# Query and key weights of the second attention in chunks for four heads, with the norm's weights applied while they are split

## The chip, the core and the metric

The kernel runs on one core of one Trainium2 chip. A core has a matrix engine (TensorE, "PE" in the profile, with its weight loads "PEld"), a vector engine (VectorE, "DVE"), a scalar engine (ScalarE, "ACT"), GpSimd ("POOL") and SyncE ("SP"), which here issues nearly all DMAs. Each engine works through its own instructions in order and waits on semaphores where it needs another's result. SBUF is the working memory of 128 partitions, and matmul results land in eight PSUM banks. The metric is the device time of one execution in microseconds.

## The reference

A trunk of two layers on 512 tokens of 1024 features: latent attention and a SwiGLU feed-forward, then chunked attention and a second feed-forward. The change touches the second attention alone. It has 16 heads of 64 features; its keys and values come from the same residual stream as its queries, under a norm with other weights:

```python
def shared_kv(x, g_src, w_kv):
    kv = (rms_norm(x, g_src) @ w_kv).reshape(B, S, 2, B_HEADS, B_HEAD_DIM)
    return gather_band(kv[:, :, 0]), gather_band(kv[:, :, 1])

def chunked_mixer(h, k_band, v_band, w_q, rel_table, w_o):   # h = rms_norm(x, attn_pre_g[1])
    q = (h @ w_q).reshape(B, n_c, CHUNK, B_HEADS, B_HEAD_DIM)
    ...
    s = jnp.einsum('bnqhd,bnkhd->bnhqk', q, k_band, preferred_element_type=jnp.float32)
    s = s * (B_HEAD_DIM ** -0.5) + bias[None, None]
    s = jnp.where(valid[None, :, None, None, :], s, -jnp.inf)
    p = jax.nn.softmax(s, axis=-1).astype(v_band.dtype)
    o = jnp.einsum('bnhqk,bnkhd->bnqhd', p, v_band).reshape(B, S, B_HEADS * B_HEAD_DIM)
    return o @ w_o
```

The norm is `x * rsqrt(mean(x^2)) * g`. The kernel multiplies the weight matrix's rows by `g` and the projection's result by the reciprocal root, so that the projections can run on `x` itself.

## The kernel before, in words

**Precision.** Every product of two float32 matrices is made of three matmuls on parts: a number is split into a high part (a cast, line 144, ScalarE) and the rest (a subtraction, line 145, VectorE), and `mm3` (lines 361 to 363) adds high x high, low x high and high x low. Where a gain goes in with the split, `split_scaled` does the same with a scaled copy and a scalar-tensor-tensor operation (lines 148 and 149).

**Weights.** `Feed` holds one list of all weight chunks of the program, up to 128 x 1024 each. A chunk is loaded by SP into one of five `raw` tiles (line 287), split into `whi` and `wlo` (three of each), and used by TensorE. `feed.next` takes the next chunk, and `feed.ahead` starts the split of the one after it. For query and key weights a chunk is one 128-feature tile of outputs over all eight input tiles of 128, so each of its eight column blocks has its own gain; line 309 multiplies the whole raw tile in place on VectorE before the split.

**The second attention.** Heads go in pairs; a pair is 128 features. `fill_b` is a generator of filler: each step, called a unit here, is one `mm3` of 512 columns for a query or key projection, or later for the output projection. A pair takes eight units for its queries and eight for its keys, then yields its number, a mark that counts as a step too. Behind the eighth unit the result is scaled by the reciprocal root (line 1582), split, and written by 4 or 8 DMAs of SP (line 1588) into the tiles `q1`, `k1` and `k2` of the pair, which lie in a ring of six.

`attention` runs 16 heads x 4 query tiles = 64 slots. Slot `i` of a head with query tile `qt` takes 128 x (`qt` + 1) keys: two score matmuls (lines 1634 and 1635, tile `sc`), one VectorE step that adds the bias and finds the minimum (line 509), and one exponential on ScalarE (line 511). Two slots later TensorE transposes the result (line 523, tile `pt`), and ScalarE and VectorE split it into `pth` and `ptl`. When a head's four tiles are there, its value product follows (lines 1642 and 1643), then `ot` and `of` (lines 1648 and 1649); after the second head of a pair the sums are turned into reciprocals, spread over a tile (`rw`, line 1654), transposed (line 1663), multiplied in and split into `oh` and `ol`. Between these steps `weave` lets the filler run up to a count: the first 12 units at slot 0, then evenly so that `units` are used up in slot 64. The filler's last part, the output projection of the attention (`out_first_b`), needs the finished pair `k` before its step `k`: three units for each of the first seven pairs inside the slots, and seven more units that are kept for behind the last scores.

The first pair's projections run ahead of the attention, between the two halves of the value projection (`plan_v`). The bias of a head is a 256 KB load on SP (line 1565) into a ring of three, begun when the head before starts, and a small memset on GpSimd.

A scheduler puts instructions of all engines in order when the program is built, so a DMA or a split can stand ahead of work written before it.

Of the kernel before, what the change touches and what calls it, by code (L numbers as in the profile page):

```python
# [18 lines left out]
D, S, P = 1024, 512, 128  # L19
# [49 lines left out]
def trunk(ctx: ExitStack, tc: tile.TileContext, a, out):  # L69
# [16 lines left out]
    def U(dt=F32, name="u"):  # L86
        return up.tile([P, S], dt, tag="u", name=name_(name), bufs=NU)
# [4 lines left out]
    def bank(tag="mm", name="b"):  # L92
        return ps.tile([P, S], F32, tag=tag, name=name_(name), bufs={"mm": 4, "s": 2, "t": 2}[tag])
# [41 lines left out]
    @contextmanager  # L135
    def first(n):

        tc.cur_priority -= n
        yield
        tc.cur_priority += n  # L140


    def split(dst_hi, dst_lo, src):
        return (nc.scalar.copy(dst_hi, src),  # L144
                V.tensor_tensor(dst_lo, src, dst_hi.bitcast(F32), op=OP.subtract))  # L145

    def split_scaled(dst_hi, dst_lo, src, col):
        return (nc.scalar.activation(dst_hi, src, AF.Copy, scale=col),
                V.scalar_tensor_tensor(dst_lo, src, col, dst_hi.bitcast(F32), op0=OP.mult, op1=OP.subtract))
# [102 lines left out]
    class Feed:  # L252
# [37 lines left out]
        def split(self, i):  # L290
            while len(self.ready) <= min(i, len(self.plan) - 1):
                j = len(self.ready)
                self.load(j + 2)
                raw, (src, n, gain, room) = self.raw[j], self.plan[j]
                for f in range(j, min(j + 8, len(self.plan))):
                    if f < j + 5 and isinstance(self.plan[f][0], Pair) or isinstance(self.plan[f][0], Down):
                        self.load(f)
                if isinstance(src, Down):
                    src.sums(*gain)
                    raw = src.at[gain]  # L300
                elif isinstance(src, Pair):
                    src.sums(gain)
                    raw = src.raw[gain]
                elif gain is not None and gain.shape[1] > 2:
                    rv = raw[:, :n].rearrange("p (a b) -> p a b", a=gain.shape[1])
                    with ExitStack() as st:
                        for b in self.behind.get(j, ()):
                            st.enter_context(tc.issue_after(b.ins))
                        V.tensor_tensor(rv, rv, gain, op=OP.mult)
                    gain = None  # L310
                if room is None:
                    at_ = 24 if isinstance(src, Pair) else 0
                    pieces = [tuple(wp.tile([P, 1152], F32R, tag=t, name=name_("w" + t), bufs=3)[:, at_:at_ + 1024]
                                    for t in ("hi", "lo"))]
                else:
                    pieces = self.room[room]()
                w = pieces[0][0].shape[1]
                if isinstance(raw, list):
                    c = 0
                    for t in raw:  # L320
                        c_ = slice(c, c + t.shape[1])
# [38 lines left out]
    def mm3(o, l, r, start, stop):  # L360
        nc.tensor.matmul(o, l[0], r[0], start=start, stop=False)  # L361
        nc.tensor.matmul(o, l[0], r[1], start=False, stop=False)  # L362
        last_mm[0] = nc.tensor.matmul(o, l[1], r[0], start=False, stop=stop)  # L363
        return last_mm[0]
# [163 lines left out]
    def attention(n_heads, start, fill, first, units, after, pace=()):  # L528


        pace = list(pace)
        slots = n_heads * NQT
        heads, done, late = {}, [0], []
        rate = (units - first) / slots

        def weave(upto):
            n = 0
            most = pace.pop(0) if fill.scored and pace else 4
            while (n < most if fill.scored else done[0] < upto) and fill.step():
                done[0] += 1  # L540
                n += 1

        for i in range(slots + 3):
            h, qt = divmod(i, NQT)
            if h < n_heads:
                if qt == 0:
                    heads[h] = start(h)
                    if h == 0:
                        weave(first)
                heads[h].scores(qt)  # L550
                fill.scored = i == slots - 1
# [12 lines left out]
        if late:  # L564
            late.pop()()
# [209 lines left out]
    plan_out(w_o[1], KT, True)  # L775
    plan_ffn(1)

# [783 lines left out]

    def bias(h):

        bt = biases[h] = pool[0].tile([P, S], F32, tag="bias", name=f"bias_{h}", bufs=3)
        nc.sync.dma_start(bt, bass.AP(tensor=rel.tensor, offset=rel.offset + h * L, ap=[[1, P], [1, S]]))
        nc.gpsimd.memset(bt[:64, :64], -BIG)

    def fill_b():
        for pr in range(H_B // 2):
            q1, k1, k2 = (pool[0].tile([P, 2, S], F32R, tag="st", name=f"{n}_{pr}", bufs=6) for n in ("q1", "k1", "k2"))  # L1570
            for t in range(2):
                b = bank()
                w = feed.next(1024, False)
                for k in range(KT):
                    if k == 3:
                        feed.ahead()
                    mm3(b, w(k * P, P), xs[k], k == 0, k == KT - 1)
                    yield True
                l = U(name="f")
                h = U(F32R, "fh")  # L1580
                with first(50):
                    V.tensor_tensor(l, b, rb, op=OP.mult)
                    split(h, l, l)
                h = h.bitcast(F32)
                for e, own in enumerate((LO, HI)):
                    for d, src, rows in (((k1, h, LO), (k1, h, HI), (k2, l, LO), (k2, l, HI)) if t else
                                         ((q1, h, LO), (q1, l, HI))):
                        nc.sync.dma_start(d[rows, e].bitcast(F32), src[own])
            qk_b[pr] = q1, k1, k2
            yield pr  # L1590
        yield from out_first_b()

    def out_first_b():
# [116 lines left out]
def _layout(i):  # L1710
# [20 lines left out]
        for f in range(2)])  # L1731
# [24 lines left out]
    o["w_qkb"] = np.stack([np.stack([_chunks(w, r(j * P, j * P + P), KT)[0] for w in (wq, wkv)])  # L1756
                           for j in range(H_B // 2)])

    w = np.clip(r(S + P - 1) - CHUNK, 0, MAX_REL + CHUNK - 1)
    o["rel"] = c(i["b_rel_table"][0][:, w])  # L1760
# [23 lines left out]
```

## Time and profile before

| | |
|---|---|
| median of three runs | 1115.44 us (1115.43 to 1116.55) |
| profiled execution, first to last instruction (its span) | 1112.9 us |
| mean granted TensorE clock | 0.998 |
| TensorE busy, matmuls | 1100.7 us, 99% |
| VectorE busy | 931.1 us, 84% |
| ScalarE busy | 685.6 us, 62% |
| first scores of the second attention | 588.8 us from the start |
| scores of its last slot | 732.9 us from the start |

The profile gives no time for the profiled execution beyond its span; the runs' times lie about 2.5 us above it. In rows of the trace, a name like `whi<-raw` is the written tile and what it is made from; "idle before" is the time the engine stood still just ahead of the instructions of a group. Matmuls overlap: the time from one start to the next is what TensorE spends on one, and its duration is longer.

### The profile page before, as it was taken

To read this page: it belongs to the slowest core of one execution; us is meant where nothing else is said; L and a number is where in the kernel's file an instruction comes from. 1 tells how busy PE (TensorE), PEld (TensorE's weight loads), DVE (VectorE), ACT (ScalarE), POOL (GpSimd) and SP (SyncE) were. 2 spreads that over 40 slices of the span, in tenths; PEclk is the share of its full clock that TensorE was granted. 3 is DMA by queue.
4 is the path that set the end of the run, shared out by engine and by line. 5 is a ranking of instruction groups with operands and counts; after the bars stand their busy time and mean duration, and the time that the engine had idled before them with its cause. 6 is when DMAs were issued, how large, how long until landed. Compare 5 with 4: busy or idle time off the path is not lost.

```text
span 1112.9 us, 18983 instructions
## 1 busy us (share of the span) xinstructions
PE 1100.7 (99%) x6973; PEld 983.8 (88%) x6973; DVE 931.1 (84%) x1671; ACT 685.6 (62%) x1339; POOL 68.5 (6%) x106
## 2 busy tenths in 40 slices
PE   9999999999999999999999999999999999999997
PEld 6888889999999998888888888889999999998885
DVE  7788737999989889978868878658999899889977
ACT  6576637755555556768636777666755555566675
POOL 1200000000000002400000000000000000002402
PEclk9999999999999999999999999999999999999999
DMA  7433226423332358970556665635422322459923
GB/s 237 117 107 81 72 72 213 133 73 108 95 125 96 126 168 240 148 213 28 186 152 170 156 181 146 152 121 176 141 76 95 133 81 97 137 170 294 172 55 77
DMA packets 62990, 150.85 MB, mean 136 GB/s; under 512 B 8432, under 2 KB 10224, under 8 KB 62896
## 3 DMA queue, kind: packets, MB, share of 16 engines
q1 hardware_dynamic: 55552, 136.61, 39.0%
q0 software_dynamic: 6912, 12.59, 6.9%
q8 instruction: 55, 0.90, 0.3%
q10 hardware_dynamic: 432, 0.44, 0.1%
q14 instruction: 39, 0.32, 0.1%
HBM read 119.52 MB, written 9.63 MB: 116 GB/s over the span
## 4 chain that ended last, share of the span: by engine, by line
PE 91%; DVE 3%; DMA 2%; issue 1%; ACT 1%; POOL 0%; SPq 0%; POOLq 0%; DVEq 0%; ACTq 0%
PE al L1487 17%; PE b L361 11%; PE b L362 11%; PE b L363 11%; PE be L1487 9%; PE al L1237 8%; PE be L1237 5%; PE ga L1487 4%; PE de L1237 3%; PE ga L1237 3%; PE pt L523 2%; DMA x<-in_x 1%; DVE wlo L145 1%; PE b L1643 1%; PE b L1642 1%
## 5 line engine op out<-in xcount | busy, mean ns | idle before, releaser
L144 ACT CAST whi<-raw 128x1024 fp32r<-128x1024 f32 (+3 forms) x224 | 225.2, 1007 | 203.8 <-PE al L1487 72.2
L145 DVE TENSOR_TENSOR wlo<-raw,whi 128x1024 fp32r<-128x1024 f32 (+3 forms) x224 | 260.6, 1165 | 52.2 <-ACT whi L144 51.3
L1487 PE MATMUL al<-th,whi 128*128 128x256 f32 x432 | 122.8, 284 | 0.2 <-DVE ut L1499 0.2
L1487 PE MATMUL al<-tl,whi 128*128 128x256 f32 x432 | 120.8, 280 | 0.0
L1487 PE MATMUL al<-th,wlo 128*128 128x256 f32 x432 | 120.8, 280 | 0.0
L361 PE MATMUL b<-xh,whi 128*128 128x512 f32 (+1 forms) x298 | 114.5, 385 | 0.0
L363 PE MATMUL b<-xh,wlo 128*128 128x512 f32 (+1 forms) x298 | 110.0, 369 | 0.3 <-DVE wlo L145 0.3
L362 PE MATMUL b<-xl,whi 128*128 128x512 f32 (+1 forms) x298 | 109.9, 369 | 0.0
L174 DVE TENSOR_TENSOR raw<-raw,raw 128x1024 f32<-128x1024 f32 x72 | 86.4, 1217 | 0.6 <-DMA raw<-in_w_pair 0.4
L1487 PEld LDWEIGHTS al<-th,whi 128*128 128x128 f32 x432 | 81.2, 188 | 2.5 <-DVE ut L1499 0.5
L1487 PEld LDWEIGHTS al<-tl,whi 128*128 128x128 f32 x432 | 81.3, 188 | 0.0
L1487 PEld LDWEIGHTS al<-th,wlo 128*128 128x128 f32 x432 | 81.2, 188 | 0.1
L511 ACT ACTIVATE p<-p,mn 128x128 f32<-128x128 f32 (+1 forms) x96 | 54.0, 562 | 39.5 <-DVE mn L509 38.6
L145 DVE TENSOR_TENSOR ptl<-pt,pth 128x128 fp32r<-128x128 f32 (+1 forms) x96 | 46.6, 486 | 29.4 <-ACT pth L144 23.6
L145 DVE TENSOR_TENSOR wlo<-wd,whi 128x512 fp32r<-128x512 f32 x86 | 56.4, 684 | 14.4 <-ACT whi L144 14.2
L144 ACT CAST whi<-wd 128x512 fp32r<-128x512 f32 x86 | 50.0, 619 | 25.5 <-PE al L1237 10.6
L363 PEld LDWEIGHTS b<-xh,wlo 128*128 128x128 f32 x298 | 56.2, 189 | 10.0 <-DVE wlo L145 0.7
L361 PEld LDWEIGHTS b<-xh,whi 128*128 128x128 f32 x298 | 56.4, 189 | 6.4 <-ACT whi L144 0.4
L362 PEld LDWEIGHTS b<-xl,whi 128*128 128x128 f32 x298 | 56.5, 189 | 5.6
L144 ACT CAST pth<-pt 128x128 fp32r<-128x128 f32 (+1 forms) x96 | 40.2, 420 | 26.9 <-PE pt L523 26.1
L1237 PE MATMUL al<-whi,ph 128*128 128x512 f32 x132 | 51.7, 392 | 0.0
L1237 PE MATMUL al<-whi,pl 128*128 128x512 f32 x132 | 51.6, 391 | 0.0
(315 smaller groups left out, 3272.0 us busy)
## 6 DMA issues: line engine op xcount, KB each, us to landing
raw<-in_w_pair SPq DMA_DIRECT2D x72, 512.0 KB, 3.7
wd<-in_w_down SPq DMA_DIRECT2D x54, 256.0 KB, 5.9
raw<-in_w_o SPq DMA_DIRECT2D x16, 512.0 KB, 3.5
raw<-in_w_gu SPq DMA_DIRECT2D x16, 512.0 KB, 3.7
raw<-in_w_down SPq DMA_DIRECT2D x16, 512.0 KB, 4.4
raw<-in_w_qkb SPq DMA_DIRECT2D x16, 512.0 KB, 3.7
wd<-in_w_down POOLq DMA_DIRECT2D x22, 256.0 KB, 5.5
wd<-raw POOLq DMA_DIRECT2D x22, 256.0 KB, 4.4
```

The source lines that it names most:

```text
L144: return (nc.scalar.copy(dst_hi, src), V.tensor_tensor(dst_lo, src, dst_hi.bitcast(F32), op=OP.subtract))
L145: V.tensor_tensor(dst_lo, src, dst_hi.bitcast(F32), op=OP.subtract))
L174: V.tensor_tensor(t, x, y, op=OP.add)
L361: nc.tensor.matmul(o, l[0], r[0], start=start, stop=False)
L362: nc.tensor.matmul(o, l[0], r[1], start=False, stop=False)
L363: last_mm[0] = nc.tensor.matmul(o, l[1], r[0], start=False, stop=stop)
L511: nc.scalar.activation(p[:, :n], p[:, :n], AF.Exp, bias=mn[:, :1], scale=-1.0, accum_out=self.sums[:, qt:qt + 1])
L523: nc.tensor.transpose(t[:, kt * P:(kt + 1) * P], p[:, kt * P:(kt + 1) * P], ident)
L1237: nc.tensor.matmul(to[e], l[c], r[d], start=j < 4 and k == 0 and n == 0, stop=k == NF // 2 - 1 and n == 2, skip_group_check=True)
L1487: nc.tensor.matmul(o, l[c], r[d], start=first_ and n == 0, stop=k == K2 - 1 and n == 2, skip_group_check=True)
L1642: nc.tensor.matmul(o[:, q_], vv, pth[:, kt, q_], start=kt == 0, stop=False)
L1643: nc.tensor.matmul(o[:, q_], vv, ptl[:, kt, q_], start=False, stop=kt == NQT - 1)
```

## The change

The query and key weights of four heads (two pairs) are laid out as four chunks: two for the queries, two for the keys, each of four input tiles of 128 by 256 output columns. A column block of 256 then has one gain, and the chunk's four blocks are split with `split_scaled` in place of line 309 and the plain split. `fill_b` makes four heads at a time with two PSUM banks, half of the input tiles per chunk. The filler before the attention is now the four heads' 32 units. The ring of `q1`, `k1`, `k2` grows from six to nine tiles, the bias ring shrinks from three to two, and the number of units given to `attention` is written as `12 + 4 * H_B * 2`, which is 140 like the number before.

```diff
-                elif gain is not None and gain.shape[1] > 2:
-                    rv = raw[:, :n].rearrange("p (a b) -> p a b", a=gain.shape[1])
...
-                        V.tensor_tensor(rv, rv, gain, op=OP.mult)
-                    gain = None
...
-                        for d in range(0, m, S):
-                            split_scaled(pieces[c // w][0][:, d:d + S], pieces[c // w][1][:, d:d + S],
-                                         raw[:, c + d:c + d + S], gain[:, (c + d) // S, 0:1])
+                        step = n // gain.shape[1]
+                        for d in range(0, m, step):
+                            split_scaled(pieces[c // w][0][:, d:d + step], pieces[c // w][1][:, d:d + step],
+                                         raw[:, c + d:c + d + step], gain[:, (c + d) // step, 0:1])
...
-    def plan_pair(pr):
+    def plan_four(n):
+        gv = gqk.rearrange("p (k t) -> p k t", t=2)
         for t in range(2):
-            feed.add(a["w_qkb"][pr, t], 1024, gqk[:, t::2].unsqueeze(2).to_broadcast([P, KT, P]))
+            for kc in range(2):
+                feed.add(a["w_qkb"][n, t, kc], 1024, gv[:, 4 * kc:4 * kc + 4, t:t + 1])
 
     plan_v(0)
-    plan_pair(0)
+    plan_four(0)
     plan_v(1)
-    for pr in range(1, H_B // 2):
-        plan_pair(pr)
+    for n in range(1, H_B // 4):
+        plan_four(n)
...
-        bt = biases[h] = pool[0].tile([P, S], F32, tag="bias", name=f"bias_{h}", bufs=3)
+        bt = biases[h] = pool[0].tile([P, S], F32, tag="bias", name=f"bias_{h}", bufs=2)
...
     def fill_b():
-        for pr in range(H_B // 2):
-            q1, k1, k2 = (pool[0].tile([P, 2, S], F32R, tag="st", name=f"{n}_{pr}", bufs=6) for n in ("q1", "k1", "k2"))
+        for n in range(H_B // 4):
+            st_ = {}
             for t in range(2):
-                b = bank()
-                w = feed.next(1024, False)
-                for k in range(KT):
-                    if k == 3:
-                        feed.ahead()
-                    mm3(b, w(k * P, P), xs[k], k == 0, k == KT - 1)
-                    yield True
...
+                b = [bank() for _ in range(2)]
+                for kc in range(2):
+                    w = feed.next(1024, False)
+                    for j in range(2):
+                        if j:
+                            feed.ahead()
+                        for kk in range(4):
+                            k = 4 * kc + kk
+                            mm3(b[j], w(kk * 256 + j * P, P), xs[k], k == 0, k == KT - 1)
+                            yield True
+                        if not kc:
+                            continue
+                        names = ("k1", "k2") if t else ("q1",)
+                        st_[t, j] = [pool[0].tile([P, 2, S], F32R, tag="st", name=f"{m}_{2 * n + j}", bufs=9)
+                                     for m in names]
...
+            for j in range(2):
+                qk_b[2 * n + j] = st_[0, j][0], *st_[1, j]
+            yield 2 * n
+            yield 2 * n + 1
         yield from out_first_b()
...
-    attention(H_B, start_b, fill, 12, 7 * 17 + 21, True, (0, 1, 1, 1, 1, 2, 4))
+    attention(H_B, start_b, fill, 12, 12 + 4 * H_B * 2, True, (0, 1, 1, 1, 1, 2, 4))
```

Two places of the instructions' order are of use. The first is TensorE late in the attention, before the change, from the scores of slot 56 (`sc_8354`) to those of slot 57; `b_8282` to `b_8284` are the banks of the output projection, that is filler, and `pt` is the transposed tile of slot 54:

```order
L1634 MATMUL sc_8354<-k_7_8038,q_7_8037 128x128
L361 MATMUL b_8284<-oh_7293,whi_8319 128x512
L1635 MATMUL sc_8354<-k_7_8039,q_7_8037 128x128
L362 MATMUL b_8284<-ol_7294,whi_8319 128x512
L363 MATMUL b_8284<-oh_7293,wlo_8320 128x512
L523 MATMUL pt_8364<-ident,p_8291 128x128 x3
L361 MATMUL b_8282<-oh_7519,whi_8198 128x512
L362 MATMUL b_8282<-ol_7520,whi_8198 128x512
L363 MATMUL b_8282<-oh_7519,wlo_8199 128x512
L1634 MATMUL sc_8373<-k_7_8038,q_7_8037 128x256
```

With the change, the same place from the scores of slot 55 (`sc_8469`) to the transposes of slot 55's result (`pt_8505`), behind the scores of slot 58; lines stand six lower:

```order
L1640 MATMUL sc_8469<-k_6_8112,q_6_7868 128x512
L1641 MATMUL sc_8469<-k_6_8113,q_6_7868 128x512
L517 MATMUL pt_8476<-ident,p_8417 128x128 x2
L1640 MATMUL sc_8485<-k_7_8183,q_7_7940 128x128
L1641 MATMUL sc_8485<-k_7_8184,q_7_7940 128x128
L517 MATMUL pt_8492<-ident,p_8443 128x128 x3
L1640 MATMUL sc_8498<-k_7_8183,q_7_7940 128x256
L1641 MATMUL sc_8498<-k_7_8184,q_7_7940 128x256
L1640 MATMUL sc_8512<-k_7_8183,q_7_7940 128x384
L1641 MATMUL sc_8512<-k_7_8184,q_7_7940 128x384
L517 MATMUL pt_8505<-ident,p_8472 128x128 x4
```

The filler between the scores is gone from slot 55 to slot 61, where the next three units stand; the number of matmuls in the whole program is the same.

The second place is VectorE in the attention, first before the change (`p` from `sc` is the slot's step at line 509, `f` a projection's result):

```order
L145 TENSOR_TENSOR wlo_6846<-raw_6704,whi_6845 128x1024
L145 TENSOR_TENSOR f_6726<-f_6726,fh_6727 128x512
L309 TENSOR_TENSOR raw_7087<-raw_7087,gains 128x1024
L509 ISA p_6758,mn_6759<-sc_6755,bias_6440 128x128
L509 ISA mn_6759 128x1
```

and with the change, around one piece of a chunk:

```order
L503 ISA p_7734,mn_7735<-sc_7731,bias_7545 128x384
L503 ISA mn_7735 128x1
L149 SCALAR_TENSOR_TENSOR wlo_7881<-raw_7600,gains,whi_7880 128x256
L145 TENSOR_TENSOR ptl_7755<-pt_7756,pth_7754 128x128
L1655 TENSOR_TENSOR of_7750<-b_7741,ot_7751 64x512
L503 ISA p_7778,mn_7779<-sc_7775,bias_7545 128x512
```

Two operations of 1024 columns became four of 256, and steps of the slots stand between them.

More of the change, by code (lines that the diff above doesn't have):

```diff
@@ L303, in split @@
                     raw = src.raw[gain]
-                elif gain is not None and gain.shape[1] > 2:
-                    rv = raw[:, :n].rearrange("p (a b) -> p a b", a=gain.shape[1])
[L306 to L309, printed above, removed]
-                    gain = None
                 if room is None:
@@ L1568, in fill_b @@
     def fill_b():
-        for pr in range(H_B // 2):
-            q1, k1, k2 = (pool[0].tile([P, 2, S], F32R, tag="st", name=f"{n}_{pr}", bufs=6) for n in ("q1", "k1", "k2"))
+        for n in range(H_B // 4):
+            st_ = {}
             for t in range(2):
-                b = bank()
-                w = feed.next(1024, False)
-                for k in range(KT):
-                    if k == 3:
-                        feed.ahead()
-                    mm3(b, w(k * P, P), xs[k], k == 0, k == KT - 1)
-                    yield True
[L1579 to L1590, printed above, removed]
+                b = [bank() for _ in range(2)]
[13 more added lines that the diff above has]
+                                     for m in names]
+                        l = U(name="f")
+                        h = U(F32R, "fh")
+                        with first(50):
+                            V.tensor_tensor(l, b[j], rb, op=OP.mult)
+                            split(h, l, l)
+                        h = h.bitcast(F32)
+                        for e, own in enumerate((LO, HI)):
+                            for d, src, rows in (((0, h, LO), (0, h, HI), (1, l, LO), (1, l, HI)) if t else
+                                                 ((0, h, LO), (0, l, HI))):
+                                nc.sync.dma_start(st_[t, j][d][rows, e].bitcast(F32), src[own])
+            for j in range(2):
+                qk_b[2 * n + j] = st_[0, j][0], *st_[1, j]
+            yield 2 * n
+            yield 2 * n + 1
@@ L1755, in _layout @@
     o["w_v"] = np.stack([_chunks(wkv, r(D + j * S, D + (j + 1) * S), 2) for j in range(2)])
-    o["w_qkb"] = np.stack([np.stack([_chunks(w, r(j * P, j * P + P), KT)[0] for w in (wq, wkv)])
-                           for j in range(H_B // 2)])
+    o["w_qkb"] = np.stack([np.stack([_chunks(w, r(j * 256, j * 256 + 256), 4) for w in (wq, wkv)])
+                           for j in range(H_B // 4)])
     w = np.clip(r(S + P - 1) - CHUNK, 0, MAX_REL + CHUNK - 1)
```

## The prediction

> **What bounds the kernel now.** I read the page first, then busy time by stage, then the groups of instructions in the second attention, then single rows of its timeline. TensorE is the bound, at full granted clock, and nearly the whole chain of waits is its own matmuls:
>
> ```profile
> PE 1100.7 (99%) x6973; PEld 983.8 (88%) x6973; DVE 931.1 (84%) x1671; ACT 685.6 (62%) x1339; POOL 68.5 (6%) x106
> ...
> PEclk9999999999999999999999999999999999999999
> ...
> PE 91%; DVE 3%; DMA 2%; issue 1%; ACT 1%; POOL 0%; SPq 0%; POOLq 0%; DVEq 0%; ACTq 0%
> ```
>
> Two stretches of the second attention show what another engine costs TensorE there (window and its length, then busy us with counts of PE, PEld, DVE, ACT, POOL; clock, DMA share, GB/s):
>
> ```profile
> 612.00:650.00 38.00, 37.32 (x207) 31.18 (x206) 31.37 (x74) 26.42 (x68) 0.58 (x4) 1.00 0.63 167
> 650.00:690.00 40.00, 39.65 (x222) 33.46 (x221) 30.67 (x76) 28.81 (x71) 0.58 (x4) 1.00 0.62 163
> ```
>
> TensorE was idle 38.00 - 37.32 = 0.68 us and 0.35 us there, and VectorE busy 83% and 77%. So VectorE work taken away is worth little unless TensorE waits for it; what TensorE lacks to do costs its full length. Both programs hold 6973 matmuls, 428 of them transposes.
>
> **TensorE's prices.** Starts set them, as durations overlap:
>
> ```profile
> 549.56 0.39 PE L361 MATMUL b<-xh,whi 128*128 128x512 f32 x1
> ...
> 551.83 0.39 PE L362 MATMUL b<-xl,whi 128*128 128x512 f32 x1
> ...
> 703.83 0.34 PE L1642 MATMUL b<-pth,vb 128*128 128x384 f32 x1
> ...
> 704.48 0.28 PE L1643 MATMUL b<-ptl,vb 128*128 128x128 f32 x1
> 704.60 0.45 PE L1634 MATMUL sc<-k,q 128*128 128x512 f32 x1
> 704.85 0.58 ACT L1648 COPY ot<-b 64x512 f32<-64x512 f32 x1 [0.21 <-PE b L1643]
> ...
> 708.21 0.49 PE L523 MATMUL pt<-ident,p 128*128 128x128 f32 x3
> ...
> 708.45 0.48 PE L361 MATMUL b<-xh,whi 128*128 128x512 f32 x1
> ...
> 708.77 0.39 PE L362 MATMUL b<-xl,whi 128*128 128x512 f32 x1
> ```
>
> Ten 512-wide matmuls start in 551.83 - 549.56 = 2.27 us: 0.23 each, and 0.68 for a filler unit of three. The pairs of 384, 256 and 128 columns take 704.60 - 703.83 = 0.77, so a head's value product (with a 512 pair, 0.45) takes 1.22, and its four score pairs, of the same sizes, 1.22. Three transposes and the slower matmul behind them take 708.77 - 708.21 = 0.56, less 0.23: 0.11 per transpose with its switch.
>
> **The change, part by part.**
>
> (1) *The scaling moves into the split.* Per chunk of 1024 columns, 16 times; groups of the stretch 500 to 660 us (count, then busy us and mean ns, then idle before):
>
> ```profile
> L309 DVE TENSOR_TENSOR raw<-raw,gains 128x1024 f32<-128x1024 f32 x16 | 19.4, 1213 | 8.9 <-DMA raw<-in_w_qkb 8.9
> ...
> L145 DVE TENSOR_TENSOR wlo<-raw,whi 128x1024 fp32r<-128x1024 f32 x13 | 15.8, 1219 | 2.1 <-ACT whi L144 2.0
> ...
> L144 ACT CAST whi<-raw 128x1024 fp32r<-128x1024 f32 x13 | 13.7, 1050 | 19.6 <-DVE raw L309 5.4 <-PE b L362 4.7 <-PE b L363 4.3
> ...
> L149 DVE SCALAR_TENSOR_TENSOR wlo<-raw,gains,whi 128x512 fp32r<-128x512 f32 x12 | 8.6, 743 | 1.9 <-ACT whi L148 1.9
> ...
> L148 ACT ACTIVATE whi<-raw,gains 128x512 fp32r<-128x512 f32 x12 | 8.1, 717 | 7.0 <-issue 3.8 <-PE b L362 2.6 <-ACT xh L144 0.6
> ...
> L145 DVE TENSOR_TENSOR xl<-x,xh 128x256 fp32r<-128x256 f32 x16 | 6.6, 415 | 0.1
> ...
> L144 ACT CAST xh<-x 128x256 fp32r<-128x256 f32 x16 | 6.2, 397 | 0.6 <-DVE x L1380 0.6
> ```
>
> Out go a 1.21 multiply, a 1.22 subtract and a 1.05 cast; in come four 256-wide scaled pairs, which no row shows. On VectorE one lies between 0.37 (half the 512-wide 0.74) and 0.74; the nearest row is the 256-wide subtract, 0.415, so I take 0.44: 1.76 for 2.43, 16 x 0.67 = 11 us less VectorE. On ScalarE between 0.36 and 0.72; nearest the 256-wide cast, 0.397; I take 0.45: 1.8 for 1.05, 12 us more ScalarE. All of it lies beside TensorE work: a chunk's eight units take 5.5 us of TensorE and its pieces 1.8. Without that cover the ScalarE excess would cost its 12 us. The short pieces also let a slot's own steps go between them. The windows' idle bounds the visible gain at 0.68 + 0.35 = 1.0 us; a wait as short as a duration beyond the pitch, 0.39 - 0.23 = 0.16, does not show as idle, and one for each of the 16 chunks would be 2.6 more. I take 0.5.
>
> (2) *Four heads at a time.* TensorE does 32 units for four heads before the attention, for 16 before. 16 x 0.68 = 10.9 us of matmuls move ahead of slot 0; they cost nothing by themselves. But the attention still spends 12 units first and (140 - 12)/64 = 2 per slot, and now holds three fours of 32 units and 2 marks, 1 mark over from the first, and 21 of the output projection: 124, not 140. It is 16 units, 8 slots, short. The order of instructions shows where: in slots 55 to 61 (from 0) stands no filler, because the three units left before the end need the finished output of heads 12 and 13, which is only made there.
>
> TensorE's own work there, from the end of head 12's value product to the first filler: scores of slots 55 to 61 (0.45 + 1.22 + 0.12 + 0.23 = 2.0), head 13's product 1.2, 20 transposes of probabilities and 4 of reciprocals at 0.11 (2.6): 5.9 us. The other engines need longer, by the groups of 592 to 708 us:
>
> ```profile
> L511 ACT ACTIVATE p<-p,mn 128x384 f32<-128x384 f32 (+3 forms) x50 | 28.3, 566 | 17.4 <-DVE mn L509 16.6 <-DMA k<-fh 0.6
> L509 DVE CUSTOM_DVE_ANT_0 p<-sc,bias 128x384 f32<-128x384 f32 (+3 forms) x50 | 24.2, 486 | 1.7 <-PE sc L1635 1.5 <-issue 0.2
> L145 DVE TENSOR_TENSOR ptl<-pt,pth 128x128 fp32r<-128x128 f32 (+3 forms) x50 | 24.0, 480 | 8.0 <-ACT p L511 4.1 <-ACT pth L144 3.9
> ...
> L144 ACT CAST pth<-pt 128x128 fp32r<-128x128 f32 (+3 forms) x50 | 20.8, 416 | 9.8 <-PE pt L523 9.2
> ...
> L511 ACT ACTIVATION_READ_ACCUMULATOR p<-p,mn 128x1 f32 x50 | 9.4, 187 | 0.0
> ...
> L1649 DVE TENSOR_TENSOR of<-b,ot 64x512 f32<-64x512 f32 x12 | 8.2, 683 | 5.9 <-ACT ot L1648 5.8
> ...
> L1648 ACT COPY ot<-b 64x512 f32<-64x512 f32 x12 | 7.0, 584 | 1.8 <-PE b L1643 1.3
> ...
> L1654 ACT COPY rw<-sums 128x256 f32<-128x256 f32 x12 | 4.2, 402 | 0.0
> ...
> L509 DVE DVE_READ_ACCUMULATOR2_ANT mn<- 128x1 f32 x50 | 4.1, 81 | 0.0
> ...
> L144 ACT CAST oh<-of 128x512 fp32r<-128x512 f32 x6 | 3.7, 623 | 0.7 <-DVE of L1664 0.7
> ```
>
> Followed in the changed order of VectorE and ScalarE: ot 0.58, of 0.68, then ptl and score step alternating (ptl 0.48 three times, score step 0.57 three times: slots 55 to 57), exponential of 57 0.75, pth 0.42 and ptl 0.48 of slot 55, head 13's product without its first matmul 1.0, ot 0.58, two rw 0.80, pth 0.42, exponential of 59 0.75, pth 0.42, oh 0.62. Sum 10.65 us. TensorE idles 10.7 - 5.9 = 4.8. Lower bound, ScalarE's occupancy alone (2 ot, 7 pth, 5 exponentials, 2 rw, oh = 9.3): 3.4. Upper, with the hand-over of 704.85 - (704.48 + 0.28) = 0.09 at 18 steps: 6.4. I take 4.8, the chain. After that the filler is back, and the 7 units kept for the end are the same in both.
>
> (3) *Buffers and queues.* q, k tiles go from 6 to 9, the bias from 3 to 2. Rows of DMA issues (page: count, KB, us to landing; by tile: ns min/median/max):
>
> ```profile
> raw<-in_w_qkb SPq DMA_DIRECT2D x16, 512.0 KB, 3.7
> ...
> L1588 SPq DMA_DIRECT2D k<-fh x28: 461/592/603, 560.8 to 695.1; - x28
> ...
> L1565 SPq DMA_DIRECT2D bias<-in_rel x16: 328/334/536, 496.4 to 706.1; - x16
> ...
> DMA to landing us min/median/max: 3.0/3.3/5.0
> ...
> L1566 POOL MEMSET bias<- 64x64 f32 x12 | 1.7, 145 | 149.3 <-DMA bias<-in_rel 118.0 <-DVE sums L1651 21.4 <-DVE f L1582 9.9
> ...
> L509 DVE CUSTOM_DVE_ANT_0 p<-sc,bias x64: 272/484/692, 590.0 to 733.7; 128x128 f32<-128x128 f32 x16, 128x256 f32<-128x256 f32 x16, 128x384 f32<-128x384 f32 x16, 128x512 f32<-128x512 f32 x16
> ```
>
> A slot takes (733.7 - 590.0)/63 = 2.3 us, four 9.1. A head's bias may now wait for the head before last and stands on SP behind up to eight q, k writes: 8 x 0.59 + 0.33 + 3.3 + 0.15 = 8.5 us of the 9.1. Covered, so nothing; in the order each q, k write waits for scores long past. Ahead of the attention SP now issues 12 more writes, 7.1 us, beside the four value chunks' 4 x 5.5 = 22 us of matmuls; the first score would be late only past that. Two of the scaled chunks now load ahead of the second half of the value chunks; loads run at least two chunks, 11 us, ahead of their use and land in 3.7, so this costs nothing.
>
> **Sum.** 4.8 - 0.5 = +4.3 us on the profiled span, 1112.9 to 1117.2. The runs' median 1115.44 lies 2.5 above the span; the same on top gives 1119.7.
>
> **The rivals.** *No change* (24%): a stall at ScalarE's bound, 3.4, and waits gone worth 1.2 or more of the 3.6 bound: 1115.4 to 1117.6. For it speaks VectorE's 83%; against it that TensorE waited for VectorE only 1.0 us in 78.
> *Faster* (10%): short pieces between the slot's steps end all 3.6 us of waits, and ScalarE and VectorE are ahead when the filler ends, so that the stretch costs 1 us: 1112.8. It decides if the empty stretch lasts under 7 us. Against: the score steps are fed by TensorE's own scores, two banks ahead at most.
> *Slower by SP* (5%): eight more writes ahead of a bias add 4.7 us to 8.5, 4.1 past the 9.1, three times, at the starts of heads 4, 8, 12; two slots in flight hide little of it: up to 12 us, 1132.
> *Slower by the clock* (3%): if the granted clock falls to half in the half-idle stretch, its 5.9 us of matmuls take up to 5.9 longer: 1125.6. The trace shows full clock in all 40 slices, with no gap as long. The longest single gap of my chain, head 13's ot and rw less two transposes, is 0.58 + 0.80 - 0.22 = 1.2 us. [...]
>
> **How the numbers follow.** My forecast holds 58%, with 8% for the two slower ones. A change under 0.2%, 2.2 us, cannot be told from none. Slower 0.66, same 0.24, faster 0.10. The range drops the faster case and the two slow tails. It starts at 1114.6, where a 3.4 stall meets all 3.6 of gain (1115.2) with 0.6 to spare, and ends at 1123.4: 6.4 without gain is 1121.8, and 1.6 is left for the 256-wide pieces at their upper ends.
>
> **What would show it.** Right: TensorE idle 4 to 6 us between head 12's and head 13's products, before it under 1; VectorE's busy time down about 11, ScalarE's up about 12; attention start 11 us later. Wrong: filler matmuls or no idle there, bias waits on VectorE at heads 4, 8, 12, a clock under 1.00, or 256-wide pieces above 0.6.

## The result, and the profile after

The changed kernel took 1121.64 us (median of four runs, 1119.93 to 1124.13), the kernel before 1115.8 us on the same chip: a ratio of 1.0052, 95% interval 1.004 to 1.0065. It is slower by about 5.8 us. The profiled execution took 1119.93 us with a span of 1118.2 us, 5.3 more than before. The page of the changed kernel:

```profile
PE 1103.2 (99%) x6973; PEld 983.7 (88%) x6973; DVE 922.2 (82%) x1703; ACT 695.6 (62%) x1387; POOL 68.6 (6%) x106
...
PEclk9999999999999999999999999999999999999999
...
PE 91%; DVE 3%; ACT 3%; DMA 1%; issue 1%; POOL 0%; SPq 0%; POOLq 0%; DVEq 0%; ACTq 0%
```

TensorE has the same 6973 matmuls at the same mean clock, 0.998. VectorE is busy 8.9 us less and ScalarE 10.0 us more, and in the chain ScalarE went from 1% to 3%. The page does not say where. The busy time by stretch does; here are the last 25 us of the attention of the kernel before (window, its length, then busy us of PE, PEld, DVE, ACT, POOL, clock, DMA share, GB/s):

```profile
720.00:745.00 25.00, 25.00 (x144) 21.39 (x144) 14.17 (x32) 14.13 (x33) 0.00 (x0) 1.00 0.18 54
```

and the same window of the changed kernel:

```profile
720.00:745.00 25.00, 22.40 (x122) 17.61 (x121) 15.71 (x46) 16.80 (x46) 0.29 (x2) 1.00 0.09 31
```

TensorE showed no idle time there before, and now shows 2.60 us. That is the part which shows as idle; a wait that ends within the overlap of two matmuls, up to 0.39 - 0.23 = 0.16 us for 512-wide ones by the prediction's rows, does not show in it. The timeline of the changed kernel in this stretch, from the end of head 12's value product to the first filler (start, duration, what; idle before it in brackets):

```profile
724.93 0.27 PE L1649 MATMUL b<-ptl,vb 128*128 128x128 f32 x1
...
725.24 0.58 ACT L1654 COPY ot<-b 64x512 f32<-64x512 f32 x1 [0.43 <-PE b L1649]
...
726.79 0.55 PE L517 MATMUL pt<-ident,p 128*128 128x128 f32 x3 [0.60 <-DVE ptl L145]
...
729.97 0.50 PE L1648 MATMUL b<-pth,vb 128*128 128x512 f32 x1
...
730.69 0.50 PE L1649 MATMUL b<-ptl,vb 128*128 128x512 f32 x1 [0.22 <-DVE ptl L145]
...
732.00 0.58 ACT L1654 COPY ot<-b 64x512 f32<-64x512 f32 x1 [1.33 <-PE b L1649]
...
732.49 0.71 ACT L1660 COPY rw<-sums 128x256 f32<-128x256 f32 x2
...
733.25 0.66 PE L1669 MATMUL rs<-ident,rw 128*128 128x128 f32 x4 [1.04 <-ACT rw L1660]
...
735.14 0.62 ACT L144 CAST oh<-of 128x512 fp32r<-128x512 f32 x1
...
735.81 0.50 PE L355 MATMUL b<-oh,whi 128*128 128x512 f32 x1 [0.32 <-ACT oh L144]
```

Head 12's product ends at 724.93 + 0.27 = 725.20 us and the next filler starts at 735.81, 10.6 us later. Between them stand the softmax steps of slots 55 to 61, head 13's value product and its reciprocals, but no filler, and every wait of TensorE that is listed is for VectorE or ScalarE.

How the rest of the 5.3 us is spread is told by first and last starts: of the scores (`sc`) and of the last reciprocals' transposes (`rs`). Kernel before, by tile, and then the changed kernel:

```profile
L1634 PE MATMUL sc<-k,q x64: 221/337/478, 588.8 to 732.9; 128*128 128x128 f32 x16, 128*128 128x256 f32 x16, 128*128 128x384 f32 x16, 128*128 128x512 f32 x16
L1663 PE MATMUL rs<-ident,rw x32: 272/273/329, 613.5 to 743.7; 128*128 128x128 f32 x32
```

```profile
L1640 PE MATMUL sc<-k,q x64: 219/337/478, 598.8 to 739.6; 128*128 128x128 f32 x16, 128*128 128x256 f32 x16, 128*128 128x384 f32 x16, 128*128 128x512 f32 x16
L1669 PE MATMUL rs<-ident,rw x32: 270/273/329, 624.3 to 749.4; 128*128 128x128 f32 x32
```

The attention starts 10.0 us later: 3672 matmuls stand ahead of its first scores in place of 3627, and 45 of them, at the 0.227 us of a 512-wide one (2.27/10 by the prediction's rows), are 10.2 us. So 15 of the 16 units went ahead of the first scores. From the first scores to the last reciprocals it lasted 743.7 - 588.8 = 154.9 us and now 150.6: 4.3 less with 44 matmuls, 10.0 us, less to do, so 5.7 us are lost inside it. 10.0 later and 4.3 shorter is 5.7 us late at its end, and 5.3 remain at the end of the span. Windows up to the end of head 12's value product and from there on divide the loss. Kernel before, and then the changed kernel:

```profile
588.80:714.62 125.82, 124.79 (x683) 104.50 (x681) 101.09 (x239) 87.81 (x220) 1.88 (x13) 1.00 0.63 165
714.62:743.68 29.06, 29.06 (x164) 24.62 (x164) 16.18 (x40) 16.76 (x42) 0.00 (x0) 1.00 0.28 78
```

```profile
598.85:725.05 126.20, 124.73 (x679) 103.36 (x678) 96.01 (x253) 91.69 (x241) 1.87 (x13) 1.00 0.60 157
725.05:749.36 24.31, 21.78 (x124) 17.30 (x123) 14.91 (x39) 15.35 (x42) 0.14 (x1) 1.00 0.14 43
```

The first window is 0.4 us longer with four matmuls (0.9 us) less, so 1.3 us are lost ahead of the empty stretch. The second is 4.75 shorter with 40 matmuls (9.1 us) less, so 4.3 are lost in the stretch and behind it.

### The profile page after: what moved, and what is told of

Read it like the earlier page. It is cut to its first block, busy times and chain, and to the rows that moved or that the text cites. A ratio compares the mean times of both kernels' runs of the same rounds, so it can differ in the third digit from the quotient of the medians.

```text
span 1118.2 us, 19059 instructions
## 1 busy us (share of the span) xinstructions
PE 1103.2 (99%) x6973; PEld 983.7 (88%) x6973; DVE 922.2 (82%) x1703; ACT 695.6 (62%) x1387; POOL 68.6 (6%) x106
## 4 chain that ended last, share of the span: by engine, by line
PE 91%; DVE 3%; ACT 3%; DMA 1%; issue 1%; POOL 0%; SPq 0%; POOLq 0%; DVEq 0%; ACTq 0%
PE al L1483 18%; PE b L355 11%; PE b L356 11%; PE b L357 10%; PE be L1483 9%; PE al L1233 8%; PE be L1233 5%; PE ga L1483 5%; PE de L1233 3%; PE ga L1233 3%; PE pt L517 2%; DMA raw<-in_w_akv 1%; PE b L1649 1%; DVE wlo L145 1%; PE b L1648 1%
## 5 line engine op out<-in xcount | busy, mean ns | idle before, releaser
L144 ACT CAST whi<-raw 128x1024 fp32r<-128x1024 f32 (+3 forms) x208 | 208.3, 1003 | 183.0 <-PE al L1483 72.6
L145 DVE TENSOR_TENSOR wlo<-raw,whi 128x1024 fp32r<-128x1024 f32 (+3 forms) x208 | 241.3, 1162 | 50.9 <-ACT whi L144 49.7
L144 ACT CAST whi<-wd 128x512 fp32r<-128x512 f32 x86 | 50.0, 619 | 25.4 <-PE al L1233 10.6
L149 DVE SCALAR_TENSOR_TENSOR wlo<-raw,gains,whi 128x256 fp32r<-128x256 f32 (+1 forms) x76 | 36.6, 521 | 20.5 <-ACT whi L148 20.4
L148 ACT ACTIVATE whi<-raw,gains 128x256 fp32r<-128x256 f32 (+1 forms) x76 | 36.9, 535 | 25.8 <-issue 12.7
```

The source lines that it names most:

```text
L144: return (nc.scalar.copy(dst_hi, src), V.tensor_tensor(dst_lo, src, dst_hi.bitcast(F32), op=OP.subtract))
```

## The experiments

**Theories.** A: the loss is the empty stretch. The filler's steady rate uses up what there is by slot 54, and in slots 55 to 61 TensorE waits for the chain of the other two engines. B: the 256-wide pieces load ScalarE. C: the two bias tiles and the longer row of writes on SP. D: the work is only in another order, and the loss lies all over the attention. Experiments 1 to 4 shared one chip, 5 to 7 another, 8 had a third and 9 a fourth, each time with the kernel before run beside them.

**1. Without the scaled pieces** (B). The changed kernel with the multiplication in place and the plain split, as before:

```diff
+                elif gain is not None and gain.shape[1] == 4:
+                    rv = raw[:, :n].rearrange("p (a b) -> p a b", a=4)
...
+                        V.tensor_tensor(rv, rv, gain.to_broadcast([P, 4, 256]), op=OP.mult)
+                    gain = None
```

> The changed kernel with the old scaling: one 1024-wide multiply on VectorE per chunk, then one plain split. Chunks, four heads, buffers and filler stay as in the change. Theory A: still 4 to 6 us slower than before, 1.004 to 1.006, with the same empty slots; part (1) is worth 1 us or less either way. Theory B: the loss goes, 1.000 to 1.001. Theory C: 1.005.

Measured: 1120.72 us (1120.21 to 1121.02), ratio 1.0054 (1.0041 to 1.0066), as slow as the change. Its page has the busy times of the kernel before:

```profile
PE 1104.5 (99%) x6973; PEld 984.8 (88%) x6973; DVE 931.5 (83%) x1671; ACT 686.1 (61%) x1339; POOL 68.3 (6%) x106
```

So the scaled pieces alone take 931.5 - 922.2 = 9.3 us from VectorE and give 9.5 us to ScalarE, and neither moves the time by as much as these runs can tell, about 1 us. B falls, and with it any gain from part (1) above that. In the trace the attention is even shorter with the old scaling; experiment 9 comes back to it.

**2. Only the 16 units ahead** (A). The kernel before, with the second pair's projections ahead of the attention and the change's buffers; chunks, scaling and the rest as before:

```diff
     plan_pair(0)
+    plan_pair(1)
     plan_v(1)
-    for pr in range(1, H_B // 2):
+    for pr in range(2, H_B // 2):
...
-    fill.until(0)
+    fill.until(1)
```

> The kernel before with one thing of the change: a second pair's 16 units run ahead of the attention, and the filler keeps its rate of 2 per slot, so it runs out 8 slots early. Query and key ring 9, bias ring 2, as in the change; scaling and chunks as before. Theory A: 4 to 6 us slower than before, 1.004 to 1.006, TensorE idle in slots 54 to 61. Theory B: no change, 1.000. Theory C: as slow as the change, but with idle time at bias waits and not in slots 54 to 61.

Measured: 1119.1 us (1118.65 to 1120.64), ratio 1.0042 (1.0029 to 1.0056): 4.3 us by the medians. The timeline shows the same waits in the same slots:

```profile
726.55 0.39 PE L1635 MATMUL sc<-k,q 128*128 128x256 f32 x1 [0.95 <-DVE mn L509]
...
732.05 0.66 PE L1664 MATMUL rs<-ident,rw 128*128 128x128 f32 x4 [1.04 <-ACT rw L1655]
...
734.61 0.97 PE L361 MATMUL b<-oh,whi 128*128 128x512 f32 x3 [0.32 <-ACT oh L144]
```

and the window of 25 us the same 2.61 us without a matmul:

```profile
720.00:745.00 25.00, 22.39 (x122) 18.08 (x123) 16.13 (x46) 16.42 (x44) 0.29 (x2) 1.00 0.06 12
```

Moving 16 units ahead makes most of the loss without any other part of the change.

**3. Only the buffers** (C). The kernel before with `bufs=9` for `st` and `bufs=2` for `bias`:

```diff
-        bt = biases[h] = pool[0].tile([P, S], F32, tag="bias", name=f"bias_{h}", bufs=3)
+        bt = biases[h] = pool[0].tile([P, S], F32, tag="bias", name=f"bias_{h}", bufs=2)
...
-            q1, k1, k2 = (pool[0].tile([P, 2, S], F32R, tag="st", name=f"{n}_{pr}", bufs=6) for n in ("q1", "k1", "k2"))
+            q1, k1, k2 = (pool[0].tile([P, 2, S], F32R, tag="st", name=f"{n}_{pr}", bufs=9) for n in ("q1", "k1", "k2"))
```

> The kernel before with the change's buffers alone: ring of q1, k1, k2 of 9, bias ring of 2. Theories A and B: no change, 0.999 to 1.001. Theory C: 1.003 to 1.005, with VectorE waiting for bias tiles.

Measured: 1114.84 us, ratio 1.0001 (0.9992 to 1.001). The buffers cost nothing. The longer row of writes on SP is not in this run; what tells of it is the row of VectorE's waits in the next section, where 2.5 of 2.6 us are for scores. By the two together C falls.

**4. The filler spread from slot 45** (A). The changed kernel with 1.2 units a slot in place of 2 behind slot 45:

```diff
+        def due(i):
+            if bend is None or i <= bend:
+                return first + rate * i
+            return first + rate * bend + slow * (i - bend)
...
-            weave(first + rate * (i + 1))
+            weave(due(i + 1))
```

> The changed kernel with one edit: behind slot 45.5 the filler is spent at 1.2 units per slot in place of 2, so that the 18 units of the output projection that can run early last into slot 60. Theory A (the empty slots 55 to 61 cost about 5 us): the stretch shrinks, the time falls by 2 to 4 us against the change, to about 1.002 of the kernel before. Theory B (the 256-wide pieces load ScalarE and cost the 5 us) and theory C (the smaller bias ring and the grouped query and key writes cost it): no change, about 1.005.

Measured: 1119.01 us (1118.05 to 1122.12), ratio 1.0043 (1.003 to 1.0056), where A had expected 1.002. The order of its instructions says why. The units came in clumps, and slots 50, 51, 55, 58 and 60 had none; of the 25 us from 720 us on, TensorE was busy for 23.41, so 1.59 us of idle time remained. A smaller rate is not an even one where a scheduler puts the units in.

**5. The changed kernel again, and three more beside it.**

> The changed kernel as it is, once more beside the three kernels that follow, so that they are compared on one chip. No theory is told apart by it: about 1.005 of the kernel before, 1120 to 1122 us.

Measured: 1121.96 us (1120.96 to 1122.19), ratio 1.0053 (1.004 to 1.0065).

**6. The last three units kept back** (A). Due counts by a table that gives out 15 units in slots 45 to 54 and keeps the sixth output tile's for slots 56 to 59:

```diff
-    attention(H_B, start_b, fill, 12, 12 + 4 * H_B * 2, True, (0, 1, 1, 1, 1, 2, 4))
+    attention(H_B, start_b, fill, 12, 12 + 4 * H_B * 2, True, (0, 1, 1, 1, 1, 2, 4),
+              lambda i: float(np.interp(i, [0, 45.5, 54.5, 57.5, 60.5, 64], [12, 103, 118, 118.5, 121, 140])))
```

> The changed kernel with its filler given out more slowly from slot 45 on (15 units in slots 45 to 54 where it has 18 in 45 to 54, and the last three units of the sixth output tile kept for slots 56 to 59). Nothing else is changed. Theory A (the attention runs out of filler in slots 55 to 61, and TensorE stands in the chain of the softmax steps): three units of 0.68 us now lie in slots that were empty, so 2 us of the idle time between head 12's and head 13's products are covered, and 2 us are won against the changed kernel: 1.003 of the kernel before. If what has to be hidden is the whole attention's chain and not its empty end, the units are missed in the slots that they leave, and nothing is won: 1.005.

Measured: 1119.84 us (1119.38 to 1120.24), ratio 1.0037 (1.0024 to 1.0049): 2.1 us under the changed kernel on the same chip, as A said. TensorE's idle time in the window goes from 2.60 to 1.59 us:

```profile
720.00:745.00 25.00, 23.41 (x131) 19.25 (x130) 16.96 (x47) 17.10 (x46) 0.29 (x2) 1.00 0.13 40
```

**7. The stretch filled with work that does nothing** (A against D). 20 matmuls with a stationary tile of zeros, added to an output bank; no value changes. In slots 55 to 58:

```diff
+    def extra(i):
+        if i == 52:
+            none.append(U(F32R, "none"))
+            nc.scalar.activation(none[0][:, :P], ident, AF.Copy, scale=zero[:, 0:1])
+        if 55 <= i <= 58:
+            for _ in range(5):
+                nc.tensor.matmul(firsts[0], none[0][:, :P], osp[0][0], start=False, stop=False, skip_group_check=True)
```

> The changed kernel with 20 more matmuls of 128x512 (0.227 us each, 4.5 us; they multiply by zeros and add to an output bank, so they change no value) in slots 55 to 58, where it has no filler; the zeros cost one ScalarE operation ahead of them. Theory A: TensorE has about 5 us idle there that a chain on VectorE and ScalarE sets, so most of these matmuls are free: at most 1.5 us over the changed kernel. Rival D (the time is lost all over the attention, as work in another order, and slots 55 to 58 are as full as others): all 4.5 us show, as in the kernel with the same matmuls in slots 48 to 51.

and the same with `if i == 45` and `if 48 <= i <= 51`:

> The same 20 matmuls of zeros in slots 48 to 51, where the changed kernel has two units of filler in each slot. Theory A: TensorE is full there and each shows, 4.5 us over the changed kernel, about 1.009 of the kernel before, less what they cover of the small waits of these slots (about 1 us). Rival D: the same as in slots 55 to 58.

Measured: 1122.52 us (1121.79 to 1123.97) in the empty slots, 0.6 over the changed kernel, and 1125.84 us (1125.33 to 1126.95) in the full ones, 3.9 over it; ratios to the kernel before 1.0062 (1.0048 to 1.0075) and 1.0092 (1.0078 to 1.0105). The same 4.5 us of matmuls (20 x 0.227) cost 3.9 us in four slots and 0.6 us in four others. TensorE's timeline of the first:

```profile
726.14 0.28 PE L1651 MATMUL b<-ptl,vb 128*128 128x128 f32 x1
...
726.99 1.41 PE L1691 MATMUL b<-oh,none 128*128 128x512 f32 x5
...
728.67 1.41 PE L1691 MATMUL b<-oh,none 128*128 128x512 f32 x5
...
730.51 1.40 PE L1691 MATMUL b<-oh,none 128*128 128x512 f32 x5
...
733.38 1.40 PE L1691 MATMUL b<-oh,none 128*128 128x512 f32 x5
...
738.08 0.96 PE L355 MATMUL b<-oh,whi 128*128 128x512 f32 x3 [0.33 <-ACT oh L144]
```

The stretch lasts 738.08 - (726.14 + 0.28) = 11.7 us where it was 10.6: 1.1 longer with 4.5 us more work in it, so 3.4 us of work went into waits. Its 25 us hold 24.55 busy ones:

```profile
720.00:745.00 25.00, 24.55 (x136) 20.38 (x136) 15.49 (x46) 15.58 (x43) 0.29 (x2) 1.00 0.12 39
```

With the matmuls in slots 48 to 51 the idle time is there as without them, 2.53 us:

```profile
720.00:745.00 25.00, 22.47 (x121) 17.80 (x121) 15.95 (x44) 15.54 (x44) 0.29 (x2) 1.00 0.13 43
```

That is A, and D falls: what counts is where TensorE has work, not how much of it.

**8. Half as many units ahead.** Experiment 2 with the second pair's queries alone:

```diff
+    plan_pair(1, (0,))
     plan_v(1)
+    plan_pair(1, (1,))
...
     fill.until(0)
+    for _ in range(8):
+        fill.step()
```

> The kernel before with only the query half of the second pair projected ahead of the attention (8 units of matmuls where the kernel with the whole second pair ahead has 16), with the nine query and key tiles and two bias tiles of the change. Theory A: the loss is what the chain leaves TensorE idle once the filler has run out, and not a price per moved unit. With 8 units fewer only slots 59 and 60 have none (54 to 60 with 16), so most of the chain of head 12 to 13 is still covered: a third of the loss of the whole pair or less, 0.5 to 1.5 us over before, ratio 1.0005 to 1.0015. Rival D (each unit that is moved ahead costs a share of its own time): half the loss of the whole pair, 2.1 to 2.4 us, ratio 1.002.

Measured: 1118.09 us (1117.44 to 1120.33), ratio 1.0021 (1.0011 to 1.003), 1.9 us by the medians. I had expected a third of the whole pair's loss or less from A (0.5 to 1.5 us), and got nearly half. By the number alone rival D, half the loss or 2.1 to 2.4 us, came nearer. The place is A's, behind the last units in slot 58 and up to slot 61, and the waits are of the same kind:

```profile
729.11 0.39 PE L1636 MATMUL sc<-k,q 128*128 128x256 f32 x1 [0.40 <-DVE mn L509]
...
730.24 0.63 PE L1665 MATMUL rs<-ident,rw 128*128 128x128 f32 x4 [0.62 <-DVE ptl L145]
...
731.73 0.63 PE L523 MATMUL pt<-ident,p 128*128 128x128 f32 x4 [0.54 <-ACT pth L144]
```

These three waits are 1.56 of the 1.57 us that TensorE is idle from 720 to 745 us. So the trace decides here for A, and the size that I gave it was wrong: two to three slots without filler are enough for waits to show. My third counted empty slots from the order and gave nothing for the half-empty slot 58.

**9. Does handling four heads at a time cost anything besides?** Experiment 2 lay 1.6 us under experiment 1 on one chip. Both have the 16 units ahead and the old scaling. They differ in how a four's units run: two tiles in turn through two banks, with both results within four units of each other. On one chip once more the changed kernel, experiment 2, and the changed kernel tile by tile:

> The changed kernel once more, on one chip with the two that follow. What is asked is whether the rest of the change, beside the 16 units ahead, costs anything: on one chip the kernel with a second pair ahead took 1119.1 us and the change with the old scaling 1120.7. About 1.005 of the kernel before.

> The kernel before with the whole second pair ahead, once more. Theory F (four heads at a time cost 1.6 us by themselves, since two banks' results come within four units of each other and their scaling, splits and writes crowd VectorE, ScalarE and SP): 1.6 us under the change on the same chip, as before. Theory G (the 16 units are all of it, and the 1.6 us were scatter between programs): within 1 us of the change.

```diff
-                b = [bank() for _ in range(2)]
-                for kc in range(2):
-                    w = feed.next(1024, False)
-                    for j in range(2):
+                w = [feed.next(1024, False) for _ in range(2)]
+                for j in range(2):
+                    b = bank()
...
+                    for k in range(KT):
+                        mm3(b, w[k // 4](k % 4 * 256 + j * P, P), xs[k], k == 0, k == KT - 1)
```

> The changed kernel with the same chunks and the same 32 units ahead, but each four's units in order of feature tiles: both chunks of the queries are taken at once, the first tile's eight units run through both, then the second's, with one bank each, so that results come eight units apart, as before the change. Theory F: 1.6 us under the change, level with the kernel with a pair ahead. Theory G: within 1 us of the change.

Measured: the changed kernel 1120.98 us (1119.72 to 1121.78, ratio 1.0046, 1.0034 to 1.0058), a pair ahead 1119.51 (1118.98 to 1122.89, ratio 1.0041, 1.0029 to 1.0054), tile by tile 1119.85 (1119.15 to 1120.37, ratio 1.0038, 1.0025 to 1.0051). The medians lie 1.5 and 1.1 us under the change, on the side of theory F, but the ranges overlap and so do the intervals. By the medians four at a time costs between nothing and some 1.5 us. The traces tell more. From the first scores to the end of head 12's product, ahead of the empty stretch, the changed kernel took 126.20, 126.25 and 126.20 us in three profiled executions. The same matmuls took 1.0 us less tile by tile, and 0.9 less in experiment 1, which has four heads at a time with the old scaling; experiment 2 is the third line:

```profile
599.56:724.76 125.20, 123.96 (x679) 103.76 (x678) 96.68 (x255) 91.91 (x244) 1.88 (x13) 1.00 0.61 158
```

```profile
599.14:724.44 125.30, 124.73 (x679) 103.34 (x678) 96.83 (x234) 86.81 (x217) 1.88 (x13) 1.00 0.61 158
```

```profile
599.99:724.40 124.41, 123.46 (x678) 103.63 (x676) 95.35 (x232) 85.77 (x217) 1.88 (x13) 1.00 0.61 159
```

So about 1 us goes when either the order of the units or the scaling is put back. Neither alone costs that much by these lines, which are one execution each; what makes the 1 us when both are there is not shown.

No kernel tried was faster than the one before.

## Why the prediction was right, step by step

The forecast was 1119.7 us; 1121.64 was measured, slower as forecast and inside the range.

**The four heads** (step 2, +4.8 us) are the cause, as predicted. The chain was worked out as 10.65 us from the end of head 12's product to the first filler and measured at 10.6; less TensorE's own 5.9 us it left 4.7 idle. That the two agree to 0.05 us is partly luck. Up to the second matmul of head 13's product the chain was worked out as 6.06 us and took 730.69 - 725.20 = 5.49, the product as 1.0 for 1.31 (to `ot` at 732.00), and the rest as 3.59 for 3.81. The sign named in advance, 4 to 6 us of idle time between head 12's and head 13's products, holds only up to the first filler and only by this subtraction: as idle the trace shows 0.82 us between the products and 2.60 in the window. The longest single wait was forecast at 1.2 us, for head 13's `ot` and `rw`, and is there with 1.04. Experiment 2 prices the step alone at 4.3 and, repeated, 3.9 us; experiments 6 and 7 show that the time is TensorE's lack of work in these slots. The windows by matmul count give 4.3 us for them.

**The scaling** (step 1) was priced right and valued wrong. Groups of 500 to 660 us of the changed kernel, each shape for itself:

```profile
L148 ACT ACTIVATE whi<-raw,gains 128x256 fp32r<-128x256 f32 x56 | 25.1, 500 | 15.3 <-issue 5.3 <-PE b L356 4.6 <-PE b L357 3.9
L149 DVE SCALAR_TENSOR_TENSOR wlo<-raw,gains,whi 128x256 fp32r<-128x256 f32 x56 | 24.5, 479 | 12.9 <-ACT whi L148 12.8
...
L149 DVE SCALAR_TENSOR_TENSOR wlo<-raw,gains,whi 128x512 fp32r<-128x512 f32 x12 | 8.5, 745 | 7.0 <-ACT whi L148 7.0
L148 ACT ACTIVATE whi<-raw,gains 128x512 fp32r<-128x512 f32 x12 | 8.1, 717 | 10.4 <-issue 7.4 <-PE b L356 2.4 <-ACT xh L144 0.6
...
L145 DVE TENSOR_TENSOR f<-f,fh 128x512 f32<-128x512 f32 x11 | 7.6, 686 | 1.4 <-ACT fh L144 1.4
...
L144 ACT CAST fh<-f 128x512 fp32r<-128x512 f32 x11 | 6.8, 617 | 5.2 <-DVE f L1586 5.2
```

A piece occupies ScalarE for 25.1/56 = 0.45 us and VectorE for 24.5/56 = 0.44, the values taken. The totals came out at -9.3 and +9.5 us (experiment 1) for -11 and +12; the 2 us between were not traced. The credit of 0.5 us for waits that would go is the part of the sum that failed: putting the old scaling back moves nothing that the medians can show, and in the traces of experiment 9 the heads ahead of the empty stretch are 0.9 us shorter with the old scaling, where the sum had 0.5 us gained by the new one. TensorE hardly waited for the VectorE work taken away, which the little idle time of the prediction's two windows, 0.68 and 0.35 us, had said already.

**Buffers and queues** (step 3, nothing) were right: ratio 1.0001. Of the 2.6 us that VectorE's steps which read the bias waited, 2.5 were for scores, in the groups of 600 to 745 us of the changed kernel:

```profile
L503 DVE CUSTOM_DVE_ANT_0 p<-sc,bias 128x256 f32<-128x256 f32 (+3 forms) x63 | 30.3, 485 | 2.6 <-PE sc L1641 2.5
```

**The sum** of 4.3 was short by some 1.0 to 1.5 us (5.3 between the spans, 5.8 between the medians). The step of four heads was close, 4.8 for 4.3. Ahead of the empty stretch 1.3 us were lost where the sum had a credit of 0.5. Experiment 2 loses nothing there (124.41 us for 678 matmuls, against 125.82 for 683 before), so the 1.3 belong to what the change has beside the 16 units. The sum had no term for that, since I looked at what the units are and how many there are, and not at two results coming together; experiment 9 finds about 1 us of it without its mechanism. In the forecast of the median, the 2.5 us between span and median held scatter too: a run's time lies 1.7 above its own span (1119.93 for 1118.2), and here the median lay 3.4 above the profiled span.

**The rivals.** *No change* is excluded, with the interval's lower end at 1.004; the stall is the chain's and not ScalarE's occupancy alone. *Faster* fell with its condition: the stretch lasted 10.6 us, not under 7. *Slower by SP* did not happen. *Slower by the clock* did not either: granted 1.00 in the window, with 1.04 us as the longest of the waits listed above. No run shows the half clock from which its 5.9 us were worked out: the mean granted clock of every run was 0.997 to 0.999.

## What to carry to other kernels

Where independent work fills another engine's waits, count it as a budget: taking units out of the loop saves nothing when the loop's own chain then stands bare, and the loss comes where the budget runs out, here in slots 55 to 61. Work out the bare chain from the durations in the groups, subtract the bound engine's own work, and test it with dummy work in the suspected slots and in full ones: here 4.5 us of it cost 0.6 us in the one place and 3.9 in the other. Taking 9.3 us from VectorE, which was 83% busy, gained nothing that could be measured here, where TensorE was idle for only 0.68 + 0.35 us in 78 us of the attention before.

## What the runs showed of the hardware

The pieces with a scale per partition took longer than the plain ones of the same width. On ScalarE a scaled 512-wide piece takes 717 ns where the cast of that width takes 617, and a 256-wide one 500 where the prediction's cast row has 397: 100 ns more at both widths. On VectorE the scalar-tensor-tensor form takes 745 for the plain subtract's 686, and 479 for the 415 of the prediction's subtract row: about 60 more. Back to back, though, the 256-wide pieces of a chunk overlap:

```profile
553.28 1.71 ACT L148 ACTIVATE whi<-raw,gains 128x256 fp32r<-128x256 f32 x4
```

```profile
553.82 1.68 DVE L149 SCALAR_TENSOR_TENSOR wlo<-raw,gains,whi 128x256 fp32r<-128x256 f32 x4 [0.55 <-ACT whi L148]
```

Four take 1.71 us on ScalarE and 1.68 on VectorE, so they start (1.71 - 0.50)/3 and (1.68 - 0.48)/3 = 0.40 us apart and overlap by about 0.10 and 0.08. The 0.45 and 0.44 us above are busy time per piece, in which the last piece of each row counts in full.
